# Up-projection weight sums made in earlier stages, a fixed engine order in the up stage, and a down stage laid into the slots that the up stage frees

## The chip, the cores and the metric

One core of one Trainium2 chip runs the whole kernel. The metric is the device time of one execution in microseconds (us). A profiled execution also has a span, from its first to its last instruction, and times inside the trace are counted from the start of that span. The engines are named as in the profile: PE is TensorE's matrix multiply and PEld its weight load, DVE is VectorE, ACT is ScalarE, POOL is GpSimd, and SP is the queue that only issues transfers.

## What is computed

One layer of a streaming encoder for 1024 prompt tokens and 8 x 16 sample tokens, together T = 1152 columns. Up to the feed-forward part:

```python
h = rms_norm(x, g_norm_mix);  z = h @ w_in              # latents, retention q k v, gates ga and gb
attn = latent_attention(...);  ret = retention(...)
merged = sigmoid(ga) * (attn @ w_oA) + sigmoid(gb) * (ret @ w_oR)
x = x + merged @ w_out
```

and the part that the change is mostly about, the convolutional feed-forward with D = 1024 and D_FF = 2816:

```python
u  = rms_norm(x, g_norm_ffn) @ w_ffn_up                 # 1024 -> 2 * 2816, gate and value halves
up = concatenate([prev, u], axis=1)                     # two earlier tokens of each sequence
c  = up[:, 0:T] * cw[0] + up[:, 1:T+1] * cw[1] + up[:, 2:T+2] * cw[2] + w['ffn_conv_b']
gate, val = c[..., :D_FF], c[..., D_FF:]
x  = x + (jax.nn.silu(gate) * val) @ w_ffn_down
```

All of it is float32. The kernel writes each operand as a rounded part `hi` and a rest `lo`, and makes a product from three matrix multiplies (hi hi, hi lo, lo hi).

## The kernel before

Features stand on the 128 partitions and tokens along the free dimension. The stages follow one another: the gates ga and gb with the first norm (lines 356 to 412), latent keys and values, retention, queries, keys and the sample tokens, prompt attention (lines 1048 to 1131, eight heads), the merge (lines 1183 to 1272: three layers `w_or`, `w_oa`, `w_out` of eight output tiles each), the up stage (lines 1278 to 1406) and the down stage (lines 1411 to 1454). Tile's scheduler puts the instructions of each engine into one fixed list before the launch: it may move an instruction ahead of others on its engine, by its own estimate of when operands and buffers are there. On the chip each list then runs in order, so an instruction that waits holds up all behind it on that engine. `tc.issue_after(i)` and `tc.add_manual_dep` bind the scheduler to an order on one engine.

`split` (line 203) makes the two parts of a tile: ACT copies `hi`, DVE subtracts `lo`.

**Attention.** For each head, POOL issues the loads of `aq`, `ak` and `av` (lines 1107 to 1110, two buffers each). PE makes scores `sc` in four banks, DVE takes maxima, ACT exponentials `ap`, DVE scales them (`L1073`), PE transposes and multiplies with the values. SP has hardly anything to issue.

**Merge.** `bslot` (line 1156) loads a weight tile into one of two raw buffers `wr` and splits it. The first weights of `w_or` depend on nothing of attention; their buffers lie where the weight pool of the stages before was.

**Up stage.** Gate tile j and value tile j form a pair, 22 pairs in all. A pair is a 2 x 2 block product done with seven block products instead of eight; `products` (line 1296) runs them in the order `p q p q r q r` over three pairs of accumulation banks, 24 matrix multiplies of 288 columns each. The seven left operands need sums of four half weights, s1 to s4. `up_w` (line 1278) loads both raw weight tiles of the next pair, has POOL make the four sums (lines 1283 to 1286), and splits seven half tiles. `read` (line 1345) takes the banks out: r1 and c11 by ACT, the others by DVE with a subtraction or an addition. After the pair `scaled` (line 1366) has POOL put the earlier tokens in, multiply by the norm's factor `ivx` and keep the last tokens; `conv` (line 1374) makes the three taps (one on ACT, two on DVE, for gate and for value), then ACT's Silu, DVE's product, and two stores of `s_act` from ACT's queue. The scheduler mixes this with the next pair's work. The second norm (line 1319) begins one step into pair 0.

**Down stage.** It has pools of its own. For each of three column groups of 384 tokens and eight output tiles, 22 k-steps of three matrix multiplies run into one bank. `down_w` loads and splits a weight tile in three pieces (two sets), `down_a` loads and splits 22 activation tiles one by one through ACT's queue.

## Time and profile before

| what | us |
|---|---|
| median of 3 runs | 2501.18 |
| fastest, slowest run | 2500.33, 2502.37 |
| the profiled execution's own time | 2497.31 |
| its span | 2495.5 |
| PE busy | 2398.6 (96%) |
| PEld busy | 2278.9 (91%) |
| DVE busy | 1488.1 (60%) |
| ACT busy | 961.9 (39%) |
| POOL busy | 605.0 (24%) |

The mean granted clock of TensorE is 0.983 of full speed. An engine's busy share here is a mean over stages with quite different limits, so the reading goes by stage: a table of stretches of the span, then the list of what PE waited for, then single instructions with their start and length. A time behind "idle before" or in square brackets is how long the engine stood idle, with the instruction that released it.

### The profile page before, as it was taken

How to read it: one execution, taken by the hardware profiler on the slowest of the kernel's cores; microseconds unless marked ns; L12 is line 12 of the kernel's file. 1: busy time of each engine (PE TensorE's matmuls, PEld its weight loads, DVE VectorE, ACT ScalarE, POOL GpSimd, SP SyncE). 2: the span in 40 equal slices, each digit the busy share in tenths (PEclk: the TensorE clock that was granted, in tenths of full speed). 3: DMA queues.
4: the chain of work that ended last, by engine and by line, in shares of the span. 5: the costliest groups of instructions: out<-in, count | busy, mean ns of one | idle time of the engine just before them, and what ended most of it. 6: DMA issues, size and time to landing. Idle time of an engine off the chain costs nothing.

```text
span 2495.5 us, 38305 instructions
## 1 busy us (share of the span) xinstructions
PE 2398.6 (96%) x14888; PEld 2278.9 (91%) x14888; DVE 1488.1 (60%) x2792; ACT 961.9 (39%) x2294; POOL 605.0 (24%) x678
## 2 busy tenths in 40 slices
PE   9999999999999999996999999999999999959999
PEld 8999998898999978885999999989999999959999
DVE  6223456546259766444886244579999998855432
ACT  5121332333246555663665022443333333344321
POOL 0001001001013212331110000237677676510000
PEclk9999999999999999998999999999999999979999
DMA  5333220111125666327674342532212222158653
GB/s 198 102 109 116 79 72 20 62 64 41 65 89 177 207 236 204 113 81 192 184 198 134 107 147 90 170 125 75 74 63 71 71 72 70 63 187 264 217 160 90
DMA packets 153893, 303.02 MB, mean 121 GB/s; under 512 B 13392, under 2 KB 88528, under 8 KB 153456
## 3 DMA queue, kind: packets, MB, share of 16 engines
q1 hardware_dynamic: 51552, 159.64, 19.7%
q10 hardware_dynamic: 74096, 88.26, 10.3%
q0 software_dynamic: 28064, 52.67, 7.5%
q8 instruction: 117, 1.92, 0.3%
q14 instruction: 64, 0.52, 0.1%
HBM read 212.47 MB, written 88.06 MB: 120 GB/s over the span
## 4 chain that ended last, share of the span: by engine, by line
PE 76%; DVE 10%; ACT 4%; DMA 4%; issue 4%; POOL 3%; ACTq 0%; SPq 0%; POOLq 0%; DVEq 0%
PE mm L188 56%; PE mm L1308 7%; PE sm L188 4%; PE sc L188 3%; POOL ug L1370 3%; PE apo L188 2%; DVE cg L1377 2%; DVE wlo L206 1%; DVE cv L1376 1%; PE apt L1085 1%; ACT whi L205 1%; DVE cg L1376 1%; ACT cg L1375 1%; DMA ar<-s_act 1%; DMA s<-s_ret 1%
## 5 line engine op out<-in xcount | busy, mean ns | idle before, releaser
L206 DVE TENSOR_TENSOR wlo<-wraw,whi 128x1024 fp32r<-128x1024 f32 (+2 forms) x165 | 232.2, 1415 | 149.9 <-ACT whi L205 149.8
L205 ACT CAST whi<-wraw 128x1024 fp32r<-128x1024 f32 (+2 forms) x165 | 162.6, 993 | 388.0 <-PE mm L188 286.1
L1308 PE MATMUL mm<-xt,whi 128*128 128x288 f32 x1408 | 287.5, 298 | 11.9 <-DVE u L1351 10.8
L188 PE MATMUL mm<-act,dh 128*128 128x384 f32 x1056 | 272.2, 338 | 26.9 <-ACT act L205 26.9
L1308 PEld LDWEIGHTS mm<-xt,whi 128*128 128x128 f32 x1408 | 224.6, 188 | 20.0 <-DVE u L1351 15.4
L188 PE MATMUL mm<-whi,xh 128*128 128x256 f32 (+2 forms) x720 | 228.4, 334 | 0.7 <-DVE gsig L365 0.7
L188 PE MATMUL mm<-whi,xl 128*128 128x256 f32 (+2 forms) x720 | 225.5, 330 | 0.0
L188 PE MATMUL mm<-wlo,xh 128*128 128x256 f32 (+2 forms) x720 | 225.0, 329 | 0.3 <-DVE wlo L206 0.3
L1308 PE MATMUL mm<-xb,whi 128*128 128x288 f32 x1056 | 215.6, 298 | 9.6 <-ACT r L1349 9.6
L188 PEld LDWEIGHTS mm<-act,dh 128*128 128x128 f32 x1056 | 192.3, 189 | 30.9 <-ACT act L205 29.2
L1308 PE MATMUL mm<-xt,wlo 128*128 128x288 f32 x704 | 207.8, 295 | 0.0
L1308 PEld LDWEIGHTS mm<-xb,whi 128*128 128x128 f32 x1056 | 170.2, 189 | 14.7 <-ACT r L1349 14.4
L188 PE MATMUL mm<-act,dl 128*128 128x384 f32 x528 | 177.2, 337 | 0.0
L1308 PE MATMUL mm<-xb,wlo 128*128 128x288 f32 x528 | 156.4, 296 | 0.0
L188 PEld LDWEIGHTS mm<-whi,xl 128*128 128x128 f32 x720 | 132.7, 190 | 12.1
L188 PEld LDWEIGHTS mm<-whi,xh 128*128 128x128 f32 x720 | 132.8, 190 | 10.5 <-issue 0.7
L188 PEld LDWEIGHTS mm<-wlo,xh 128*128 128x128 f32 x720 | 132.8, 190 | 9.8 <-DVE wlo L206 0.5
L206 DVE TENSOR_TENSOR dl<-dr,dh 128x1024 fp32r<-128x1024 f32 (+1 forms) x72 | 81.5, 1136 | 94.1 <-ACT dh L205 90.0
L188 PE MATMUL mm<-rh,whi 128*128 128x384 f32 x576 | 131.9, 336 | 2.0 <-ACT rh L205 2.0
L188 PE MATMUL mm<-rl,whi 128*128 128x384 f32 x576 | 132.1, 336 | 0.4 <-DVE rl L206 0.4
L1308 PEld LDWEIGHTS mm<-xt,wlo 128*128 128x128 f32 x704 | 132.3, 188 | 0.1
L188 PE MATMUL mm<-rh,wlo 128*128 128x384 f32 x576 | 131.5, 335 | 0.0
(481 smaller groups left out, 5787.7 us busy)
## 6 DMA issues: line engine op xcount, KB each, us to landing
dr<-w_dn SPq DMA_DIRECT2D x48, 512.0 KB, 3.6
wraw<-w_up SPq DMA_DIRECT2D x44, 512.0 KB, 3.4
s_q<-uqT ACTq DMA_DIRECT2D x36, 384.0 KB, 3.1
ar<-s_act ACTq DMA_DIRECT2D x66, 192.0 KB, 3.6
aq<-s_q POOLq DMA_DIRECT2D x8, 1536.0 KB, 8.7
s_act<-cv ACTq DMA_DIRECT2D x22, 512.0 KB, 2.6
s_gate<-gsig ACTq DMA_DIRECT2D x16, 576.0 KB, 4.8
mg<-s_gate POOLq DMA_DIRECT2D x16, 576.0 KB, 4.7
```

Of the source, the lines that this page charges most:

```text
L188: E.matmul(out, l, r, start=start, stop=stop)
L205: A.copy(hi, src)
L206: return V.tensor_tensor(out=lo, in0=src, in1=hi.bitcast(F32), op=ALU.subtract)
L1085: E.transpose(pt[:, j * 256 + e * P:j * 256 + (e + 1) * P], pm[e][:, jj * P:(jj + 1) * P], ident)
L1308: E.matmul(banks[bank][c], l[:, ks], x, start=bool(first) and k + e == 0, stop=k + e == 5, skip_group_check=not first)
L1370: G.tensor_tensor(out=u[:, 2:], in0=u[:, 2:], in1=ivx[:, 2:], op=ALU.mult)
L1375: A.activation(c, u[:, 2:], AF.Identity, scale=gc(C_CW, 2 * NF + f), bias=gc(C_CB, f))
L1376: V.scalar_tensor_tensor(out=c, in0=u[:, 1:NU - 1], scalar=gc(C_CW, NF + f), in1=c, op0=ALU.mult, op1=ALU.add)
L1377: V.scalar_tensor_tensor(out=c, in0=u[:, 0:NU - 2], scalar=gc(C_CW, f), in1=c, op0=ALU.mult, op1=ALU.add)
```

## The change

- `presum(j, pool, bufs)` loads the two raw up weights of pair j from SP's queue, makes the four sums on POOL, and stores them to a new scratch tensor `s_w[j]` (1 MB each) from POOL's queue. Pairs 0 to 10 are made in the gate stage, one per gate tile 2 to 12 with two buffers; pairs 11 to 21 in attention, one or two per head, with one buffer for each raw tile.
- `up_raw` loads the finished sums beside the raw weights into four raw buffers of their own; the up stage makes no sums.
- The second norm starts after product 4 of pair 0 instead of near its beginning.
- From pair 1 on, `in_order` chains ACT's, DVE's and POOL's instructions in the order in which they are written. The convolution of pair j-1 is written into the products of pair j. Multiplying by `ivx` moves from POOL to DVE, in three pieces, and into the reading of c11, which moves from ACT to DVE.
- `s_act` holds three pairs in a tile and is stored from SP's queue.
- The splits of the first two `w_or` weights are bound behind the last ACT and DVE instructions of head 5.
- The down stage takes slots of the up stage. In the last pair it loads and splits its first weights and activations; the first two output tiles run side by side, k-step by k-step; the rest of the last pair's convolution is written between their splits, in a fixed order. Activations are loaded three at a time from POOL's queue.

```diff
+        def presum(j, p, bufs):
+            rg, rv = (p.tile([P, D], F32, name=n, bufs=bufs) for n in ("prg", "prv"))
+            S.dma_start(rg, d["w_up"][j])
+            S.dma_start(rv, d["w_up"][NJ + j])
+            s = p.tile([P, 4, 512], F32, name="psum", bufs=2)
+            u, v = slice(0, 512), slice(512, D)
+            G.tensor_tensor(out=s[:, 1], in0=rg[:, u], in1=rv[:, u], op=ALU.add)
...
+            G.dma_start(s_w[j], s)
...
                     gate_out(f, fm_tile(mm, wslot(d["w_gate"][f], D), xr))
+                    presum(f - 2, wk, 2)
...
+                for j in range(11 + 11 * h // H, 11 + 11 * (h + 1) // H):
+                    presum(j, wk, 1)
...
+                if h == H - 3:
+                    anchors = [next(i for i in reversed(nc.cur_bb.bb.instructions) if i.engine == e) for e in (mybir.EngineType.Activation, mybir.EngineType.DVE)]
...
-            wts = [bslot(d[w][f]) for f in (f0, f1)]
+            with ExitStack() as block:
+                if not turn[0]:
+                    for i in anchors:
+                        block.enter_context(tc.issue_after(i))
+                wts = [bslot(d[w][f]) for f in (f0, f1)]
...
+        def up_raw(j):
+            return [wraw(0, d["w_up"][j]), wraw(1, s_w[j][:, 0:2]), wraw(2, s_w[j][:, 2], d["w_up"][NJ + j][:, 512:]), wraw(3, s_w[j][:, 3])]
...
+            def then(n, ps):
+                g, v = j - 1, NJ + j - 1
+                if n == 0:
+                    me.read_p(ps)
+                    if prev:
+                        prev.keep(g, prev.ug)
+                        prev.tap(v, prev.uv, prev.cv, 1)
+                elif n == 1:
+                    me.read_u2(ps)
+                    if prev:
+                        prev.tap(v, prev.uv, prev.cv, 0)
+                        prev.tap(g, prev.ug, prev.cg, 1)
+                        prev.tap(g, prev.ug, prev.cg, 0)
+                        A.activation(prev.cg, prev.cg, AF.Silu)
+                    if last:
+                        me.ra = [act_raw(0, i) for i in range(3)]
+                elif n == 2:
+                    me.read_c11(ps)
+                    if last:
+                        wa.extend(down_w(0, 0, set_a))
+                    else:
+                        prep(0)
+                    if prev:
+                        prev.product()
+                elif n == 3:
+                    me.read_u3(ps)
...
+                        prep(1)
+                elif n == 4:
+                    me.read_c22(ps)
+                    me.past(NJ + j, me.uv)
+                    if j:
+                        me.scale(me.uv, A2)
...
+                elif n == 5:
+                    me.read_c21(ps)
+                    if j:
+                        me.scale(me.uv, A1)
+                        me.keep(NJ + j, me.uv)
+                        me.cv = me.tap2(NJ + j, me.uv, "cv")
...
+                        prep(2)
                 else:
+                    me.read_c12(ps)
+                    me.past(j, me.ug)
+                    if j:
+                        me.scale(me.ug, A2)
+                        me.cg = me.tap2(j, me.ug, "cg")
+                    if not last:
+                        prep(3)
...
+            with in_order():
+                prev.keep(j, prev.ug)
+                acts += act_split(prev.ra[2], act_tiles(AT[2]))
+                ra = [act_raw(0, i) for i in (3, 4)]
+                prev.tap(v, prev.uv, prev.cv, 1)
+                prev.tap(v, prev.uv, prev.cv, 0)
+                wa += down_w(0, 1, set_a)
+                prev.tap(j, prev.ug, prev.cg, 1)
+                prev.tap(j, prev.ug, prev.cg, 0)
+                A.activation(prev.cg, prev.cg, AF.Silu)
+                wb += down_w(1, 1, set_b)
+                acts += act_split(ra[0], act_tiles(AT[3]))
+                ra += [act_raw(0, i) for i in (5, 6)]
+                prev.product()
...
+            for k in range(NJ):
+                for q, ww in zip(ps, (wa, wb)):
+                    mm3(q, ww[k], acts[k], k == 0, k == NJ - 1)
```

`tap` is one DVE tap of 1168 columns, `tap2` ACT's tap with the bias, `prep(i)` the split of the next pair's raw tile i (1024, 1024, 1024 and 512 columns), `scale` the multiplication by `ivx`, `past` and `keep` small POOL copies of the earlier and the last tokens.

## Rows read from the trace of the kernel before

**Rows 1.** What PE waited for, whole span: total us, times, longest.

```profile
PE mm L188 <- ACT act L205: 26.9, 5, 24.9
PE sc L188 <- ACT ap L1069: 14.8, 2, 14.2
PE mm L1308 <- DVE u L1351: 10.8, 20, 0.6
PE mm L1308 <- ACT r L1349: 9.6, 21, 1.7
PE sm L315 <- DVE acc L1234: 5.0, 1, 5.0
```

**Rows 2.** Stretches: A:B, length, PE, PEld, DVE, ACT, POOL busy, PEclk, DMA share, GB/s.

```profile
0.00:40.00 40.00, 37.00 (x200) 35.35 (x201) 26.80 (x28) 28.17 (x30) 1.13 (x6) 1.00 0.64 214
914.50:917.90 3.40, 3.40 (x15) 3.30 (x16) 1.66 (x4) 1.50 (x6) 0.98 (x1) 0.50 0.62 196
1190.00:1337.00 147.00, 147.00 (x1060) 139.43 (x1058) 122.79 (x395) 94.17 (x286) 19.48 (x24) 1.00 0.63 169
1640.00:1684.00 44.00, 37.97 (x242) 36.53 (x241) 34.10 (x48) 20.02 (x31) 16.95 (x14) 0.88 0.25 80
1700.00:2160.00 460.00, 440.96 (x3229) 429.53 (x3228) 416.98 (x425) 164.89 (x210) 327.56 (x268) 1.00 0.20 69
2072.00:2076.00 4.00, 2.35 (x18) 2.12 (x18) 3.80 (x4) 1.64 (x2) 3.94 (x6) 1.00 0.08 31
2184.00:2240.00 56.00, 29.13 (x136) 25.36 (x136) 27.98 (x37) 22.23 (x32) 6.46 (x9) 0.73 0.57 180
2240.00:2490.00 250.00, 250.00 (x1442) 249.54 (x1441) 106.24 (x133) 82.11 (x109) 11.27 (x21) 1.00 0.61 188
```

**Rows 3.** By line, shapes apart: least/median/longest ns, or busy us and mean ns.

```profile
L1377 DVE SCALAR_TENSOR_TENSOR cv<-uv,c_gcol,cv x22: 1430/3901/3908, 1686.0 to 2187.6; 128x1168 f32<-128x1168 f32 x22
L1375 ACT ACTIVATE cv<-uv,c_gcol x22: 1360/1366/1369, 1682.2 to 2184.5; 128x1168 f32<-128x1168 f32 x22
L1283 POOL TENSOR_TENSOR wsum<-wraw x22: 1287/2421/2431, 1614.7 to 2145.6; 128x512 f32<-128x512 f32 x22
L206 DVE TENSOR_TENSOR wlo<-wraw,whi 128x1024 fp32r<-128x1024 f32 x8 | 9.7, 1218 | 6.0 <-ACT whi L205 6.0
L205 ACT CAST whi<-wraw 128x1024 fp32r<-128x1024 f32 x40 | 42.0, 1051 | 56.2 <-PE mm L1308 56.2
```

**Rows 4.** In order of time, the start of attention: start, length, instruction.

```profile
1159.00 1.04 ACT L205 CAST whi<-wraw 128x1024 fp32r<-128x1024 f32 x1 [10.28 <-DMA s_att<-wraw]
1163.52 1.23 DVE L206 TENSOR_TENSOR wlo<-wraw,whi 128x1024 fp32r<-128x1024 f32 x1 [2.22 <-ACT whi L205]
```

**Rows 5.** In order of time, ACT's Silu in pairs 1 and 21.

```profile
1694.00 1.18 ACT L1399 ACTIVATE cg<-cg 128x1168 f32<-128x1168 f32 x1 [2.34 <-DVE cg L1377]
2172.46 1.18 ACT L1399 ACTIVATE cg<-cg 128x1168 f32<-128x1168 f32 x1 [2.97 <-DVE cg L1377]
```

**Rows 6.** In order of time, PE within a pair of the up stage.

```profile
1812.41 0.29 PE L1308 MATMUL mm<-xt,wlo 128*128 128x288 f32 x1
1812.81 0.29 PE L1308 MATMUL mm<-xt,wlo 128*128 128x288 f32 x1
1813.63 0.53 PE L1308 MATMUL mm<-xt,whi 128*128 128x288 f32 x2 [0.53 <-DVE u L1351]
```

**Rows 7.** In order of time, DVE reading banks one behind the other.

```profile
1796.70 0.44 DVE L1338 TENSOR_TENSOR uv<-u,mm 128x288 f32<-128x288 f32 x1
1797.07 0.31 DVE L1341 TENSOR_TENSOR uv<-u,mm 128x160 f32<-128x160 f32 x1
1797.30 0.28 DVE L1343 TENSOR_TENSOR uv<-u,mm 128x128 f32<-128x128 f32 x1
```

**Rows 8.** By line, attention 1190 to 1337: one shape of the scaling.

```profile
L1073 DVE TENSOR_SCALAR ap<-ap,ast 128x1024 f32<-128x1024 f32 x7 | 5.5, 780 | 0.0
```

**Rows 9.** In order of time, PE ahead of the second stretch of rows 2.

```profile
914.34 0.44 PE L188 MATMUL sm<-vh,sl 128*128 128x256 f32 x1 [1.51 <-DVE sl L206]
```

More of the change, by code (lines that the diff above doesn't have):

```diff
@@ L201, in behind, with __enter__, __exit__ @@
         return block
+    class in_order:
+        def __enter__(self):
+            self.at = len(nc.cur_bb.bb.instructions)
+        def __exit__(self, *_):
+            traced = nc.cur_bb.bb.instructions
+            for e in (mybir.EngineType.Activation, mybir.EngineType.DVE, mybir.EngineType.Pool):
+                last = None
+                for n, i in enumerate(traced):
+                    if i.engine != e:
+                        continue
+                    if n >= self.at and last is not None:
+                        tc.add_manual_dep(i, last.name, mybir.DependencyInfo(mybir.DependencyClass.NoSync, mybir.DependencyReason.DATA), reason="in_order")
+                    last = i
     def split(hi, lo, src, scale=None):
@@ L316, in col_sums @@
             return ps[:, :NT]
+        def presum(j, p, bufs):
[5 more added lines that the diff above has]
+            G.tensor_tensor(out=s[:, 1], in0=rg[:, u], in1=rv[:, u], op=ALU.add)
+            G.tensor_tensor(out=s[:, 2], in0=rv[:, u], in1=rv[:, v], op=ALU.add)
+            G.tensor_tensor(out=s[:, 0], in0=s[:, 2], in1=rg[:, u], op=ALU.add)
+            G.tensor_tensor(out=s[:, 3], in0=s[:, 0], in1=rg[:, v], op=ALU.add)
+            G.dma_start(s_w[j], s)
         warm = ExitStack()
@@ L1308, in products @@
                             E.matmul(banks[bank][c], l[:, ks], x, start=bool(first) and k + e == 0, stop=k + e == 5, skip_group_check=not first)
-                    read(n, c, banks[bank][c])
-                stream.tick()
+                then(n, banks[bank])
         us = ExitStack()
@@ L1379, in _body @@
-        w = up_w(0)
-        stream.now = 0
-        nrm = norm()
-        def later():
-            yield 1
-            yield from nrm
-        stream.start(later())
-        for j in range(NJ):
-            ug, uv = up(j, w)
-            stream.drain()
-            if j < NJ - 1:
-                w = up_w(j + 1)
-            scaled(NJ + j, uv)
-            cv = wk.tile([P, NU - 2], F32, name="cv")
-            conv(NJ + j, uv, cv)
-            scaled(j, ug)
-            cg = wk.tile([P, NU - 2], F32, name="cg")
-            conv(j, ug, cg)
-            A.activation(cg, cg, AF.Silu)
-            V.tensor_tensor(out=cv[:, :SEQ], in0=cg[:, :SEQ], in1=cv[:, :SEQ], op=ALU.mult)
-            sa = wk.tile([P, NB * NS], F32, name="sa")
-            sv = lambda a: a[:, SEQ:].rearrange("p (b c) -> p b c", c=NS + 2)[:, :, 2:]
-            V.tensor_tensor(out=sa.rearrange("p (b i) -> p b i", b=NB), in0=sv(cg), in1=sv(cv), op=ALU.mult)
-            A.dma_start(s_act[j][:, :SEQ], cv[:, :SEQ])
-            A.dma_start(s_act[j][:, SEQ:], sa)
@@ new lines, in act_split, with act_tiles @@
+        def act_split(r, two):
+            n = r.shape[1]
+            hi, lo = (t.rearrange("p (a c) -> p a c", a=3)[:, :n] for t in two)
+            split(hi, lo, r)
+            return [(hi[:, i], lo[:, i]) for i in range(n)]
+        def act_tiles(tags):
+            return [slots.tile([P, T], F32R, name="act", tag=t) for t in tags]
+        AT = [(5, 6), (7, 8), (9, 10), (13, 14), (15, 16), (19, 20), (21, 22), (23, 24)]
+        AT = [tuple(DS[i] for i in t) for t in AT]
+        raw_w = up_raw(0)
```

305 lines of the change are left out of this document (193 added, 112 removed).

## The prediction

> **What bounds the kernel now.** I read the table of stretches first, then the list of what PE waited for, then single instructions. PE is busy in 96% of the span, so a change can win only where PE stands still or runs at its lower clock. The list of waits puts most of that into two places: 26.9 us for the down stage's first activations and 14.8 us for attention's exponentials [rows 1]. The up stage adds 20.4 us in small waits, one for r1 and one for u2 in each pair, and the second norm 5.0 us [rows 1]. In the table attention and the down stage hold PE busy throughout at full clock, while 2184 to 2240 has 136 matrix multiplies and a clock of 0.73, and 1640 to 1684 a clock of 0.88 [rows 2]. In the up stage DVE is as full as PE, 417 of 460 us, because POOL is busy 328 us beside it [rows 2]: the same DVE tap takes 1.43 us at least and 3.90 us in the median, POOL's addition 1.29 and 2.42 [rows 3]. The longer ones are those that meet the other engine.
>
> **Start of attention.** ACT's copy of a `w_or` weight waited 10.3 us for a transfer that waited for the store of `s_att` [rows 4]. Its partner on DVE ended at 1164.75, and attention's first maxima and exponentials stand behind both; hence PE's 14.2 us. Binding these splits behind head 5 removes that, and their cover there is two heads of full PE work. The third weight of `w_or` is not bound and could still stand in front, for one load and one split (about 4 us, estimated from the 1.05 and 1.22 of its parts and a load). I take 12 us won, between 8 and 17 (the whole wait, and some 2 us of lower clock behind it).
>
> **Up to down.** In 2184 to 2240, 136 multiplies at 250/1442 = 0.173 us are worth 23.6 us; 32 us are lost [rows 2]. Afterwards PE can start at once: the first weights and six activations are split within the last pair. The two outputs side by side use a k-step in 6 x 0.173 = 1.04 us, so k = 8 is wanted 8.3 us after the last up product. What is needed then stands in a fixed order on DVE and ACT: reading c12 and scaling (1.8), ACT's tap (1.37), activation group 2 (1.16 and 1.36, by columns from 1.05 and 1.22), two taps, a weight piece, two taps (2.8, 1.15, 2.8), Silu (1.18), the other piece (1.05 and 1.22): 15.9 us, with some 2 us that DVE is behind, and then activations 9 to 11 (1.4). That is 19 us against the 9.4 at which k = 9 is wanted. So about 11 us are lost in waits, and 2.7 more at the lower clock. Won: 32 - 13.5 = 18.5 us, between 12 and 27. The conv_new store, the POOL-issued activation loads and the y stores ride beside 12 us of multiplies per output, as now.
>
> **Merge to up.** `col_sums` no longer stands in front of PE at 5.0 us [rows 1]; the norm's work itself stays and goes between products 4 to 6 and pair 1, where scaling and ACT's taps of pair 0 hold r1 of pair 1 for 1 to 2 us. I take 4 won, 1 to 7.
>
> **Up stage.** A pair takes (2172.46 - 1694.00)/20 = 23.92 us [rows 5]. PE's own pace is three multiplies in 0.40 us, 56 x 0.398 = 22.3 [rows 6]. Without POOL's sums and scalings DVE's operations fall to their least times, but they stand in a fixed order now. Per pair: four taps 5.72 [rows 3]; eight bank reads of 0.44 and two sets of 0.44 + 0.31 + 0.28 [rows 7], 5.58, c11 among them; three scalings of 576 to 592 columns, about 0.76 each between 128 and 1024 columns, 2.28; four rests 3 x 1.22 + 0.68, 4.34 [rows 3]; the product 1.5. Together 19.4, less 0.07 where an operation starts before the one ahead has ended [rows 7], about 1.4: 18.0 us. In that order DVE waits three times for ACT. Behind the last tap: Silu 1.18 and a copy 1.05, less the reading of c11, 1.5. Behind the second scaling: ACT's tap 1.37 and a copy 1.05, 2.4. Behind the third: 1.37 and 0.6, 2.0 [rows 3, 5]. That is 5.9 and 0.2 for the steps between engines: 24.1 us a pair. So the stage goes from DVE with POOL to a loop through DVE and ACT, and PE waits once a pair, about 1.8 us, at product 5 for u3, instead of twice. Behind DVE's waiting subtraction stand the reads of c12 and u3, and PE for their banks. 21 pairs at +0.15: 3 us lost, between 28 won (PE's pace) and 10 lost (the loop 0.5 us longer). POOL's copies fit in DVE's waits; s_act on SP's queue and four loads a pair meet a DMA share of 0.20 [rows 2].
>
> **Sums in the gate stage.** 44 POOL additions and 22 MB of transfers move here. SP waits for raw buffers after the first x rows, so I expect the first four loads (2.1 MB, buffers are free from the start) ahead of the later x rows in SP's queue. The stretch 0 to 40 moves 214 GB/s at a share of 0.64 [rows 2], so 2.1 MB are some 6 us of the full rate, and the additions (1.29 each) meet DVE, which splits x for PE. Bounds: nothing, if PE's rows come in time; 14 for both. I take 6, nearer to the transfers. The stage behind it has DVE mostly free, and a gate tile of 72 multiplies lasts 12.5 us.
>
> **Sums in attention.** PE is full there and DVE busy 122.8 of 147 us [rows 2]. 44 additions of 1.29 us are on POOL 57 of 190 us. The 64 scalings (1024 columns in 0.78 us [rows 8]) and as many tiny two-input operations of the softmax may each meet one with a chance of 0.3 and wait half of it: 25 us of DVE at most, which would fill it to 97%. The transfers add 23 MB in 190 us, 121 GB/s; at the down stage's 0.61 for 188 GB/s [rows 2] that is 0.39 beside 0.63: the queues would be full, and POOL's loads of the next heads share them. They have a whole head, 22 us, to come. Bounds 0 and 25; I take 7, nearer to PE's full rows.
>
> The Trainium skill says on this (SBUF — State Buffer, section "SBUF: two separate sides") that DVE, with two SBUF inputs or in a two-port mode, and GpSimd hold a shared port pair as "an exclusive lock, not a bandwidth split", for a whole instruction. The trace agrees: 3.90 against 1.43 us. By that rule alone the up stage would fall to PE's pace and attention would pay the full 25 us; the sum would be 2466 for the execution.
>
> **Sum.** 2497.3 - 12 - 18.5 - 4 + 3 + 6 + 7 = 2478.8 for an execution like the profiled one; the median of the runs is 3.9 above that execution, so 2482.7; I give 2482.
>
> **Rivals.**
> - *The up stage reaches PE's pace.* For it: DVE's 18.0 us of work fit in 22.3, and the scheduler may still move PE and SP. Against it: ACT's and DVE's orders are fixed, and the three waits stand in the text. 22.3 to 22.6 a pair: 31 us less than the forecast, 2452.
> - *Slower: PE's one wait drops the clock.* A wait of 1.5 us was followed by 3.4 us at 0.50, the 1.2 GHz level [rows 2, 9]; one of 1.7 us in the up stage was not, the clock stayed at 1.00, 2.4 GHz [rows 1, 2]. With 1.8 us in every pair it could go either way. 3.4 us at half clock cost 1.7 us a pair, 36 in all: 2519. It decides from about 15 pairs of 21.
> - *The sums cost what they save.* Gate and attention at their upper ends, 39 us instead of 13: 2509. For it: a full DMA share and a full DVE. Against it: none of this is needed before the up stage.
> - *The bound splits don't free attention*, since other work is put in front of it: 12 us back, 2495.
>
> **How the numbers follow.** The forecast has 0.55, PE's pace 0.13, the clock 0.11, the costly sums 0.16, the missing anchor 0.05. The forecast's own range is 2466 to 2497. To leave out no more than 0.2 the range goes down to PE's pace, 2451, and up to the costly sums, 2508. About 0.2%, 5 us, is what a measurement can tell from no change. Faster: nearly all of the forecast, PE's pace, and half of the missing anchor, 0.70. Same, 2496 to 2506: half of the costly sums, half of the missing anchor and the forecast's upper end, 0.13. Slower: the clock and the rest of the sums, 0.17.
>
> **What would show it.** Right: no wait of PE near 1150 us; a wait of 5 to 8 us some 9 us into the down stage and full rows after; Silu every 24 us; DVE's taps at 1.43; one PE wait for u3 per pair. Wrong: a period of 22.5 (DVE not the loop), a PEclk under 1.00 between 1700 and 2160, waits for x rows in the first 30 us above 14, or scores waiting for `ak` and `aq` in attention.

## The result and the profile after

The changed kernel takes 2513.0 us (median of 4 runs, 2511.9 to 2515.4) against 2500.8 us before: a ratio of 1.005, interval 1.0032 to 1.0067. It is slower by 0.5%, where 2482 us were forecast. Its profiled execution took 2511.9 us, 14.6 more than the one of before.

Where that came from is seen first in the positions of a few TensorE instructions, in us from the start of the span. (The last column is the start of the last multiply of the down stage. The lower rows belong to experiments below.)

| kernel | end of the kv stage | first score | end of attention | first up product | last down product |
|---|---|---|---|---|---|
| before | 241.8 | 1148.1 | 1341.1 | 1645.5 | 2491.6 |
| after | 259.0 | 1166.1 | 1367.8 | 1671.6 | 2506.0 |
| no sums in the gate stage | 244.2 | 1153.8 | 1355.0 | 1660.7 | 2492.9 |
| no sums in attention | 258.6 | 1166.0 | 1351.6 | 1657.0 | 2489.7 |
| gate sums, transfers alone | 256.1 | 1163.2 | 1365.1 | 1669.9 | 2500.9 |
| gate sums held back | 249.0 | 1159.0 | 1361.4 | 1665.7 | 2500.4 |
| taps moved | 260.5 | 1168.8 | 1367.6 | 1672.4 | 2457.8 |
| no order, sums late | 246.7 | 1164.6 | 1342.1 | 1647.3 | 2424.3 |

So the changed kernel is 17.2 us behind when the kv stage ends, and between there and the first score it loses only 0.8 more. Attention takes 201.6 us instead of 192.9. From the end of attention on it is faster by 12.3.

From the list of what PE waited for, whole span, columns as in [rows 1]:

```profile
PE mm L1342 <- ACT whi L222: 18.8, 19, 1.0
PE mm L1342 <- DVE wlo L223: 8.8, 19, 0.5
PE sc L188 <- ACT ap L1101: 7.4, 2, 5.2
PE mm L188 <- DVE gsig L396: 6.4, 4, 5.0
PE sm L327 <- DVE diag L324: 6.0, 1, 6.0
PE apo L188 <- DVE apT L223: 5.4, 11, 0.6
PE mm L188 <- ACT dwhi L222: 4.5, 1, 4.5
PE mm L188 <- ACT act L222: 3.6, 2, 3.0
PE apo L188 <- DMA av<-s_v: 3.6, 2, 2.4
```

The two large lines of [rows 1] have shrunk: the down stage's activations from 26.9 to 3.6 and 4.5 (weights), attention's exponentials from 14.8 to 7.4. New are the two single waits of the gate stage, of 5.0 and 6.0 us, the small ones in attention, and one line that was not in the forecast: 19 waits of 1.0 us for the copy of the next pair's weights in the up stage.

Four stretches that answer to [rows 2], by stage and moved with the work, and the stretch 40 to 90 beside them:

```profile
0.00:40.00 40.00, 34.78 (x177) 32.59 (x178) 31.75 (x23) 25.07 (x27) 19.40 (x15) 0.96 0.76 267
40.00:90.00 50.00, 39.03 (x204) 36.55 (x203) 24.08 (x31) 12.41 (x13) 35.05 (x30) 0.90 0.93 355
1215.00:1362.00 147.00, 140.01 (x971) 131.09 (x971) 126.95 (x367) 88.10 (x267) 60.90 (x59) 0.98 0.91 277
1725.00:2185.00 460.00, 432.63 (x3180) 422.88 (x3179) 341.13 (x510) 148.36 (x171) 43.16 (x152) 1.00 0.31 101
2205.00:2261.00 56.00, 44.98 (x240) 42.20 (x239) 40.71 (x47) 25.88 (x26) 11.53 (x21) 0.88 0.61 208
```

In the up stage POOL fell from 328 to 43 busy us in 460, DVE from 417 to 341, and yet PE starts 3180 multiplies where it started 3229. In the seam to the down stage PE has 240 multiplies in 56 us instead of 136. The first two lines show the price of the gate's sums. The fullest transfers of that stage are not in its first 40 us but behind them, 355 GB/s at a share of 0.93, and there PE is busy 39 of 50 us, at a clock of 0.90.

Two single waits of PE, of 6.0 and 5.0 us, are all that is missing there. In order of time on SP, ACT, DVE, POOL and PE (start, length, instruction, in brackets the idle time ahead of it and what ended it):

```profile
11.54 0.75 SPq L339 DMA_DIRECT2D prg<-w_up  x1
13.67 0.65 SPq L340 DMA_DIRECT2D prv<-w_up  x1
39.55 1.51 SPq L282 DMA_DIRECT2D wraw<-w_gate  x3
46.66 1.04 ACT L222 CAST whi<-wraw 128x1024 fp32r<-128x1024 f32 x1 [9.37 <-DMA wraw<-w_gate]
47.73 1.22 DVE L223 TENSOR_TENSOR wlo<-wraw,whi 128x1024 fp32r<-128x1024 f32 x1 [6.44 <-ACT whi L222]
49.13 1.83 POOL L278 TENSOR_TENSOR inv<-ss,negh 128x9 f32<-128x9 f32 x1 [2.82 <-DVE ss L434]
51.81 1.65 PE L327 MATMUL sm<-diag,ones 128*128 128x384 f32 x2 [5.98 <-DVE diag L324]
54.45 2.75 DVE L324 TENSOR_SCALAR diag<-ident,inv 128x128 f32<-128x128 f32 x3
64.19 2.31 DVE L223 TENSOR_TENSOR wlo<-wraw,whi 128x1024 fp32r<-128x1024 f32 x1
78.89 1.49 DVE L396 TENSOR_TENSOR gsig<-mm,ivb 128x384 f32<-128x384 f32 x3 [10.36 <-DMA s_gate<-gsig]
79.50 1.61 PE L188 MATMUL mm<-xh,whi 128*128 128x384 f32 x3 [4.99 <-DVE gsig L396]
```

The first four loads of the sums were issued at 11.5 to 13.7 us, ahead of later x rows, as forecast; that cost some 3 us (the norm's first column sum starts at 40.4 instead of 37.4). The wait of 6.0 us came from SP's queue. After 30.7 SP waited 8.4 us to issue a load of the sums, because its tile was still read by POOL's additions, which took 2.1 to 2.4 us each beside DVE's work instead of 1.29 [rows 3]; the loads of the next gate weights stood behind it and went out from 39.55 on. ACT's copy of such a weight waited for its load until 46.66, DVE's rest for that copy, and DVE's reading of the norm's column sums, ready since 42.6, stood behind that rest until 48.88. POOL itself was idle then, and its `inv` took 1.83 us. Behind it DVE's diagonals and rests take two to four times their length beside the next additions (2.31 instead of 1.22 [rows 3]), and DVE waits 10.4 us until a store of `s_gate` gives its tile back, with PE behind it.

### The profile page after: what moved, and what is told of

Its sections match the earlier page's. It is cut to its first block, busy times and chain, and to the rows that moved or that the text cites. A ratio compares the mean times of both kernels' runs of the same rounds, so it can differ in the third digit from the quotient of the medians.

```text
span 2510.1 us, 38500 instructions
## 1 busy us (share of the span) xinstructions
PE 2406.2 (96%) x14888; PEld 2284.6 (91%) x14888; DVE 1441.6 (57%) x2857; ACT 938.8 (37%) x2210; POOL 436.1 (17%) x679
## 4 chain that ended last, share of the span: by engine, by line
PE 68%; DVE 15%; DMA 6%; issue 5%; ACT 4%; POOL 2%; ACTq 0%; SPq 0%; DVEq 0%; POOLq 0%
PE mm L188 54%; PE mm L1342 5%; PE sm L188 4%; DVE wlo L223 3%; ACT whi L222 2%; DVE cg L1432 2%; DVE cv L1432 2%; DMA prg<-w_up 2%; PE sc L188 1%; PE apo L188 1%; DVE ug L1420 1%; DMA prv<-w_up 1%; DVE uv L1420 1%; DVE u L1381 1%; DMA ak<-s_k 0%
## 5 line engine op out<-in xcount | busy, mean ns | idle before, releaser
L223 DVE TENSOR_TENSOR wlo<-wraw,whi 128x1024 fp32r<-128x1024 f32 (+4 forms) x223 | 261.3, 1178 | 312.0 <-ACT whi L222 310.9
L222 ACT CAST whi<-wraw 128x1024 fp32r<-128x1024 f32 (+4 forms) x223 | 217.9, 993 | 416.9 <-PE mm L188 349.8
L188 PE MATMUL mm<-act,whi 128*128 128x384 f32 x528 | 136.2, 337 | 4.6 <-ACT act L222 3.6
L188 PE MATMUL mm<-act,dwhi 128*128 128x384 f32 x528 | 135.7, 336 | 4.5 <-ACT dwhi L222 4.5
L188 PE MATMUL mm<-xh,whi 128*128 128x384 f32 x528 | 125.1, 343 | 8.7 <-DVE gsig L396 5.7
L188 PE MATMUL mm<-xl,whi 128*128 128x384 f32 x528 | 122.3, 337 | 1.1 <-DVE xl L226 1.1
```

The source lines that it names most:

```text
L188: E.matmul(out, l, r, start=start, stop=stop)
L222: A.copy(hi, src)
L223: return V.tensor_tensor(out=lo, in0=src, in1=hi.bitcast(F32), op=ALU.subtract)
```

## The experiments

Each was made from the changed kernel unless it says otherwise, and its ratio is to the kernel before, run beside it on the same chip.

### Without the gate's sums, without attention's

```diff
-                    presum(f - 2, wk, 2)
...
+            q = j % 11 + 11
-            return [wraw(0, d["w_up"][j]), wraw(1, s_w[j][:, 0:2]), wraw(2, s_w[j][:, 2], d["w_up"][NJ + j][:, 512:]), wraw(3, s_w[j][:, 3])]
+            return [wraw(0, d["w_up"][j]), wraw(1, s_w[q][:, 0:2]), wraw(2, s_w[q][:, 2], d["w_up"][NJ + j][:, 512:]), wraw(3, s_w[q][:, 3])]
```

> The changed kernel without the eleven sets of sums of the gate stage; pairs 0 to 10 of the up stage read the sums of pairs 11 to 21 instead, so the up stage has the same loads and the same work but other numbers. Theory 'the sums cost what they save' (stage boundaries after the gate stage stand 17 us later in the changed kernel than before): the kernel gets 14 to 19 us faster, 2494 to 2499 us, and the boundary at the end of the kv stage falls back to that of the kernel before within 2 us. Rival 'the shift comes from the order in which the scheduler put the gate stage's own work, not from the sums': under 5 us, 2508 to 2513.

Measured: 2494.6 us, ratio 0.9977 (0.9968 to 0.9986). The kv stage ends at 244.2, 2.5 us from before (2 were forecast).

```diff
-                for j in range(11 + 11 * h // H, 11 + 11 * (h + 1) // H):
-                    presum(j, wk, 1)
...
+            q = j % 11
```

> The changed kernel without the eleven sets of sums of the attention stage; pairs 11 to 21 read the sums of pairs 0 to 10. Theory 'the sums stand in the way of attention' (its body lost some 15 us, its start won 6): 10 to 20 us faster, 2493 to 2503 us, and the start of attention wins the 12 us that the forecast gave it, because the head transfers of the sums no longer stand beside it. Rival 'attention lost to the anchored weight loads and the third split that is bound to nothing': within 3 us, 2510 to 2516.

Measured: 2495.9 us, 0.9985 (0.9975 to 0.9995). Attention takes 185.6 us: 16.0 less than with the sums, but only 7.3 less than before. So the sums cost 18 and 17 us of the whole time, 35 if the two add up, and the first theory held in both; that the start of attention would get back its 12 us did not come true. Something else stands there.

### What of the sums it is, in the gate stage

```diff
+            if j < 11:
+                G.dma_start(s_w[j][:, 0:2], rg)
+                G.dma_start(s_w[j][:, 2:4], rv)
+                return
             s = p.tile([P, 4, 512], F32, name="psum", bufs=2)
```

> The changed kernel with the gate stage's sums reduced to their transfers: the same two loads, and stores of the same 8 KB per partition taken straight from the loaded tiles, with no addition on POOL (so pairs 0 to 10 multiply other numbers). Theory 'transfers': the loads at 11 to 14 us push the x rows back and fill the queue, and the 17 us stay within 4 us, 2509 to 2513 us. Rival 'the shared port of DVE and POOL': the additions alternate with DVE's row splits and evacuations, and most of it goes, 10 to 16 us, 2497 to 2503.

Measured: 2506.6 us, 1.0023 (1.0013 to 1.0034): 6 us won, between the two forecasts, 2.9 of them up to the end of the kv stage. Transfers alone keep 14.3 of the 17.2 us there, but not at the same places. The stretch 40 to 90, and DVE behind it in order of time:

```profile
40.00:90.00 50.00, 49.21 (x282) 47.32 (x281) 16.55 (x32) 14.77 (x15) 7.75 (x12) 1.00 0.96 361
111.34 0.76 DVE L462 TENSOR_TENSOR c_cos<-c_cos,c_grow 128x576 f32<-128x576 f32 x1 [27.40 <-DMA c_grow<-grow]
112.69 1.48 DVE L400 TENSOR_TENSOR gsig<-mm,ivb 128x384 f32<-128x384 f32 x3
```

In 40 to 90 PE now loses almost nothing, with as many bytes as in the changed kernel (361 and 355 GB/s): the two waits there need the additions as well. The constants that the kv stage multiplies are loaded from SP's queue too. DVE came to them early in its own order, waited 27.4 us for their transfer, and the gate's evacuation stood behind it; PE waited 6.8 us. That the loss is one of waiting in order was not what I had expected. How much of the 17 us belongs to the bytes and how much to the additions this run does not tell, since the waits moved; and the edit does one thing more: a tile that is stored as it was loaded is free only when its store has landed.

```diff
-                    presum(f - 2, wk, 2)
+                    with behind():
+                        presum(f - 2, wk, 2, A)     # loads from ACT's queue
```

> The changed kernel with each set of the gate stage's sums loaded from ACT's queue behind that gate tile's sigmoid, so that the first loads start after the norm instead of at 11 us; the same sums, the same number of bytes. Theory 'it is where they start': the 17 us shrink to 0 to 5, 2496 to 2501 us, with no gap of PE above 2 us between 50 and 90 us. Rival 'the sums cost this wherever they lie in this stage': over 10 of the 17 us stay, 2506 to 2513.

Measured: 2499.8 us, 1.0007 (0.9995 to 1.0019), 13 us won with the same bytes and the same additions. The stretch 40 to 90 is whole again, and a new wait stands at 201.6, of DVE and PE in order of time:

```profile
40.00:90.00 50.00, 49.35 (x284) 48.23 (x284) 16.70 (x31) 12.53 (x13) 16.03 (x11) 1.00 0.62 214
199.70 0.76 DVE L459 TENSOR_TENSOR c_cos<-c_cos,c_grow 128x576 f32<-128x576 f32 x1 [3.29 <-DMA c_grow<-grow]
201.61 0.40 PE L188 MATMUL mm<-whi,xh 128*128 128x288 f32 x1 [3.27 <-DVE ckv L475]
```

So most of the cost was in where the loads stand, as the theory had it. The edit changes two things at once, when the loads start and whose queue they are in: SP's queue no longer waits for POOL ahead of a gate weight. Which of the two did it is not separated. What remains lies at the end of the gate stage, where SP waits 7.3 us for the last additions ahead of a load of the kv stage's constants, and DVE for such a transfer.

### What of the sums it is, in attention

```diff
+            if j >= 11:
+                G.dma_start(s_w[j][:, 0:2], rg)
+                G.dma_start(s_w[j][:, 2:4], rv)
+                return
```

> The changed kernel with the attention stage's sums reduced to their transfers: the same two loads, and stores of the same bytes straight from the loaded tiles, no addition on POOL (so pairs 11 to 21 multiply other numbers). Without any of it the stage won 17 us. Theory 'the transfers fill the queues' (the heads' own loads and the first weights come late, as in the gate stage, where the transfers alone kept 14 of 17 us): under 5 us are won, 2508 to 2513 us. Rival 'the shared port': DVE is busy for 88 % of this stage and each addition shuts it out, so 10 to 16 us are won, 2497 to 2503 us.

Measured: 2520.4 us, 1.008 (1.006 to 1.010): without the additions it is 7 us slower than with them, which neither forecast had. What PE waited for between 1185 and 1375:

```profile
PE sc L188 <- DMA aq<-s_q: 8.2, 1, 8.2
PE sc L188 <- DMA ak<-s_k: 3.4, 1, 3.4
PE apo L188 <- DMA av<-s_v: 2.4, 1, 2.4
```

In the changed kernel the same list has 5.0 us for `apT`, in ten waits, and 4.0 for `av` and `ak`. The additions therefore cost PE some 5 us through DVE (0.3 us are left here); but without them 14 us are waited for the heads' own loads. These are issued from POOL's queue, behind whatever waits there for a load of the sums: an addition in the changed kernel (first fence), a store in this one (second).

```profile
1290.89 1.28 POOL L343 TENSOR_TENSOR psum<-prg,prv 128x512 f32<-128x512 f32 x1 [6.16 <-DMA prg<-w_up]
1295.67 1.81 POOL L1142 DMA_DIRECT2D av<-s_v  x2
```

```profile
1288.34 0.56 POOL L342 DMA_DIRECT2D s_w<-prg  x1 [8.43 <-DMA prg<-w_up]
1289.59 0.77 POOL L1143 DMA_DIRECT2D aq<-s_q  x1
```

Between 1185 and 1310 POOL waited 111 us for loads of the sums in this run and 48 in the changed kernel. As in the gate stage, a tile is held here until its store has landed, so the loads themselves are not the same in time, and why the run is slower than with the additions is not settled.

To tell the queue from the bandwidth, the same bytes with the stores from SP:

```diff
-                G.dma_start(s_w[j][:, 0:2], rg)
-                G.dma_start(s_w[j][:, 2:4], rv)
+                S.dma_start(s_w[j][:, 0:2], rg)
+                S.dma_start(s_w[j][:, 2:4], rv)
```

> As the run with attention's sums reduced to their transfers, with the stores issued from SP's queue instead of POOL's: the same bytes, but POOL's queue, from which the heads' own loads are issued, never waits for a load of the sums. (Pairs 11 to 21 multiply other numbers.) Against that run's 2520 us. Theory 'queue order': the waits for aq, ak and av (14 us in that run) go, and the time falls by 10 to 18 us, 2502 to 2510 us. Rival 'bandwidth': the queues of the transfer engines are full in this stage, and the heads' loads stay late, 2516 to 2523 us.

Measured: 2522.4 us, 1.0088 (1.0071 to 1.0105). By the time the rival holds, by the trace neither. No wait for `aq`, `ak` or `av` is left. In their place PE waits 16.7 us for ACT's `apT` and 11.9 for ACT's `aat`, and ACT waits, between 1160 and 1260:

```profile
ACT whi L222 <- DMA wraw<-w_or: 17.0, 1, 17.0
ACT ap L1105 <- DMA prv<-w_up: 15.2, 1, 15.2
```

The first is the third weight of the merge, whose load is now queued on SP behind the stores that wait. The second names a load of the sums; ahead of it ACT issued a store of `s_att` (at 1249.28, after 14.9 us without an instruction), and what held that is not settled. So moving the 11.5 MB of stores to another queue moved the wait to whoever shares that queue. How much of attention's 16 us would stay if nothing stood behind the sums in any queue, these runs do not say.

### The start of attention

```diff
-                ps = fm_tile(mm, bslot(d[w][f]), rows) if i > 1 else first[i]
+                if i > 1:
+                    with bound():          # behind the anchors while turn[0] < 3
+                        wt = bslot(d[w][f])
+                ps = fm_tile(mm, wt, rows) if i > 1 else first[i]
...
+        with bound(99):
             w = [wtile(r, r.shape[1], i) for i, r in enumerate(raw_w)]
```

> The changed kernel with the third weight split of the merge and the first pair's four splits bound to the same two instructions of head 5 as the first two. In the changed kernel the third split stands on ACT ahead of attention's first exponential and waits 6.0 us for its weights. Theory 'that one split is what is left of the wait at the start of attention': TensorE's 5.6 us gap there shrinks to at most 1.5, and with the half clock behind it 6 to 9 us are won, 2504 to 2507 us. Rival 'the transfers of attention's sums are late anyway': under 2 us, 2511 to 2514 us.

Measured: 2506.7 us, 1.0030 (1.0018 to 1.0041), 6 us won. On ACT in order of time, first the changed kernel (its two splits are the third weight of `w_or` and the last of the first pair), then this one:

```profile
1172.67 1.71 ACT L222 CAST whi<-wraw 128x1024 fp32r<-128x1024 f32 x2 [5.96 <-DMA wraw<-w_or]
1174.28 0.36 ACT L1101 ACTIVATE ap<-sc,ast 128x128 f32<-128x128 f32 x1
```

```profile
1169.28 0.37 ACT L1101 ACTIVATE ap<-sc,ast 128x128 f32<-128x128 f32 x1 [0.93 <-DVE ast L1094]
```

PE's gap in the scores goes from 5.2 to 1.1 us, and the time is in the range of the theory. Attention as a whole gets 2.9 us shorter in the two profiles (198.7 us): a wait of 3.6 us for `ak`, and two stretches of 6.8 us at the 1.2 GHz level (a granted clock of 0.50), took part of it back. The other side of the test, the kernel before with nothing but the three splits bound:

```diff
-            wts = [bslot(d[w][f]) for f in (f0, f1)]
+            with bound():
+                wts = [bslot(d[w][f]) for f in (f0, f1)]
```

> The kernel before with only one part of the change, extended by its missing third: the first three weight splits of the merge bound behind head 5. The forecast gave 12 us, between 8 and 17. Theory 'the wait at the start of attention is those splits and nothing else': 12 to 15 us won against the kernel before, 2485 to 2489 us. Rival 'the first scores wait for something else next' (as with the changed kernel's sums left out, where 7 us came of it): 5 to 9 us, 2491 to 2496 us.

Measured: 2487.7 us, 0.9947 (0.9932 to 0.9962), 13.5 us won; attention falls from 192.9 to 178.2 us, and no wait of PE above 1 us is left between the first score and 1190. The theory holds: the splits were the whole wait, and all three must be bound.

### The up stage

The period from Silu to Silu, over 20 pairs, is (2206.7 - 1719.7)/20 = 24.35 us in the changed kernel (23.92 before [rows 5]). By line, shortest/median/longest ns and first and last start:

```profile
L1515 ACT ACTIVATE cg<-cg x21: 1179/1180/1182, 1719.7 to 2206.7; 128x1168 f32<-128x1168 f32 x21
```

One pair, in order of time, on PE, ACT and DVE:

```profile
1794.82 0.80 PE L1342 MATMUL mm<-xb,whi 128*128 128x288 f32 x4 [0.99 <-ACT whi L222]
1796.08 0.40 PE L1342 MATMUL mm<-xb,wlo 128*128 128x288 f32 x1 [0.47 <-DVE wlo L223]
1792.65 1.18 ACT L1515 ACTIVATE cg<-cg 128x1168 f32<-128x1168 f32 x1 [6.40 <-DVE cg L1432]
1793.74 1.98 ACT L222 CAST whi<-wraw 128x1024 fp32r<-128x1024 f32 x2
1805.09 1.23 DVE L223 TENSOR_TENSOR wlo<-wraw,whi 128x1024 fp32r<-128x1024 f32 x1 [2.41 <-ACT whi L222]
1809.99 0.69 DVE L223 TENSOR_TENSOR wlo<-wraw,whi 128x512 fp32r<-128x512 f32 x1 [2.00 <-ACT whi L222]
1810.60 1.43 DVE L1432 SCALAR_TENSOR_TENSOR cv<-uv,c_gcol,cv 128x1168 f32<-128x1168 f32 x1
```

The taps have their 1.43 us, and DVE waits for ACT where it was forecast, 2.4 and 2.0 us. PE however waits for the next pair's weights: the written order binds ACT, DVE and POOL, and the scheduler placed 18 of the next pair's 24 first multiplies ahead of this pair's last two products.

```diff
-                for e in (mybir.EngineType.Activation, mybir.EngineType.DVE, mybir.EngineType.Pool):
+                for e in (mybir.EngineType.Activation, mybir.EngineType.DVE, mybir.EngineType.Pool, mybir.EngineType.PE):
```

> The changed kernel with the written order of the up stage fixed for TensorE too, and nothing else. In the changed kernel the scheduler put 18 of the next pair's first 24 matmuls ahead of this pair's last two products, and TensorE waits there 1.0 us for the copy of the next weights. Theory 'the loop of DVE and ACT sets the period': the wait of 1.3 us moves to the reads of the next pair, the period stays between 24.0 and 24.4 us and the time within 6 us, 2507 to 2515. Rival 'TensorE's order sets the period': it falls to 22.5 to 23.0 us, and the time by 27 to 38, 2475 to 2486 us.

Measured: 2512.7 us, 1.0050 (1.0033 to 1.0066), the same as the changed kernel. PE between 1740 and 2140:

```profile
PE mm L1342 <- DVE u L1381: 26.9, 16, 1.9
```

Now PE waits once a pair for u3, 1.7 us, just as the forecast said, and the period is 24.27. PE's order decides where it waits, not how long the pair is. The loop itself:

```diff
 # product 0 of the next pair
-                        prev.tap(v, prev.uv, prev.cv, 1)
 # product 1
-                        prev.tap(v, prev.uv, prev.cv, 0)
...
-                        A.activation(prev.cg, prev.cg, AF.Silu)
 # product 2, behind prep(0)
+                        A.activation(prev.cg, prev.cg, AF.Silu)
 # product 6 of the own pair, behind the tap on ACT
+                        me.tap(NJ + j, me.uv, me.cv, 1)
+                        me.tap(NJ + j, me.uv, me.cv, 0)
```

> The changed kernel with DVE's two taps of the value half moved from the head of the next pair to the end of its own pair, where DVE waits 2.0 us for ACT, and the copy of the next weights put ahead of Silu on ACT. Same work. Theory 'the period is the loop from the last read of a pair over the scaling, ACT's tap, DVE's four taps and Silu to the next weights': the loop loses 2.7 us and the period falls to TensorE's own, 22.3 to 22.7 us, 2472 to 2482 us. Rival 'something else sets it' (the exclusive port, or the weights' transfers): above 23.9 us a pair, 2503 to 2513 us.

Measured: 2464.7 us, 0.9860 (0.9846 to 0.9875), 48 us won, more than the theory's range; it beats both kernels. And the order taken away altogether:

```diff
-                    if n >= self.at and last is not None:
+                    if n < 0:
```

> The changed kernel with the written engine order of the up stage and of its tail taken away: the scheduler places the same work. The forecast's term for the up stage was 24.1 us a pair with the order written out; measured 24.30. Theory 'the written order is what lengthens the pair': the scheduler moves the value half's taps into DVE's idle time by itself, as the moved taps did by hand, and the period falls to 22.4 to 23.2 us, 2470 to 2490 us. Rival 'the order costs nothing, the sums' removal had already made the loop': 23.9 to 24.5 us, 2506 to 2518 us.

Measured: 2459.5 us, 0.9837 (0.9813 to 0.9861), again more than forecast. The stretch 1725 to 2150 of the changed kernel, of the taps moved, and of no order, each in its own fence:

```profile
1725.00:2150.00 425.00, 400.17 (x2944) 391.36 (x2943) 314.84 (x473) 136.23 (x156) 39.48 (x142) 1.00 0.32 102
```

```profile
1725.00:2150.00 425.00, 425.00 (x3210) 425.00 (x3209) 345.98 (x520) 152.06 (x171) 51.31 (x156) 1.00 0.34 111
```

```profile
1725.00:2150.00 425.00, 425.00 (x3210) 425.00 (x3209) 352.33 (x520) 159.69 (x172) 68.09 (x152) 1.00 0.34 111
```

In both PE has no gap left: 425 us hold 3210 multiplies, and 425/3210 x 168 = 22.2 us for a pair. The written order, not the work, was the limit of the changed up stage. With DVE's taps at the head of the next pair, each pair runs through the last read, the scaling, ACT's tap, four taps and Silu before the next weights are copied, 24.3 us in all; two taps moved into DVE's wait of 2.0 us, and Silu put behind the copy, take the loop under PE's own pace. (The run makes both moves, so their shares are not known.)

The order cost something behind the pairs too. From the same multiply of the last pair to the last one of the down stage, the kernel with the taps moved takes 298.0 us and the one without the order 289.7. There PE has no wait above 0.4 us, at a clock of 1.00; with the order it waited 3.6 us for a piece of a down weight, and the clock stood at 0.50 for 6.8 us behind it.

### The sums somewhere else

```diff
-                    presum(f - 2, wk, 2)
+                    if f < 12:
+                        with behind():
+                            presum(f - 2, wk, 2, A)
...
+                    for hf in range(2):                      # query latents
+                        with behind():
+                            presum_half(10 + f, hf, wk, A)
...
+                    for hf in range(2):                      # first layer of the merge
+                        with behind():
+                            presum_half(todo[0], hf, wk, A)
```

> The changed kernel with the same 22 sets of sums made elsewhere: ten in the gate stage, loaded from ACT's queue behind each gate tile's sigmoid from the third tile on; six in halves in the stage of the query latents; six in halves under the first layer of the merge; none in the attention stage. Theory 'the cost of the sums is that of the place': gate 0 to 5 us instead of 17, attention the 16 back, 2480 to 2490 us. Rival 'their 63 MB and 88 additions cost the same wherever they lie': above 2505 us.

Measured: 2580.9 us, 1.0320 (1.0303 to 1.0337), the worst of all, though attention took 184.3 us. PE waited for these, among others:

```profile
PE mm L188 <- ACT rh L222: 25.0, 3, 16.8
PE mm L188 <- DVE upn L736: 23.8, 1, 23.8
776.50 0.28 ACT L725 ACTIVATE usq<-mm 128x128 f32<-128x128 f32 x1 [32.88 <-DMA s_w<-prg]
```

With single buffers an addition on POOL waits for each load, and a load on ACT's queue until the store of the half before has landed. The 23.8 us for `upn`, from 762 on, show both: ACT's squares for that tile stood behind such loads until 776.5 (the last line, a row of ACT in time), and then POOL's powers until 783.8, behind a half whose first addition had waited 5.2 us for `prg`. The time lies in the rival's open range, but 68 us above the changed kernel is not "the same", and neither theory had this: here the cost hung less on the bytes, or on a stage being idle, than on what is queued behind each wait.

```diff
+            V.tensor_tensor(out=s[:, v], in0=rg[:, u], in1=rv[:, u], op=ALU.add)   # additions on DVE
...
+                    with behind():
+                        nxt = presum(f - 2, wk, A)         # loads behind this gate tile
+                        next(nxt)
+                    if f > 2:
+                        next(held_sum)                      # additions one tile later
...
+                        if t in (0, 3) and todo:            # retention stage, raw weight buffers
+                            mine = presum_in(todo.pop(0))
```

and, with it, the moved taps and the bound splits of above.

> Everything that the earlier runs point to, in one kernel: the taps moved and the weights' copy ahead of Silu in the up stage, the third split and the first pair's splits bound, the sums of pairs 0 to 10 in the gate stage with loads from ACT's queue behind each gate tile and additions on DVE one tile later, those of pairs 11 to 21 in the retention stage, through the weights' own raw buffers, additions on DVE. Theory 'three separate causes that add up': the taps' 48 us, the split's 6, 14 to 17 of the gate's and 16 to 17 of attention's: 2424 to 2436 us. Rival 'the sums cost in the retention stage too', because its weight loads share the three buffers and the queue: 10 to 25 us more, 2436 to 2455 us.

Measured: 2450.6 us, 0.9803 (0.9783 to 0.9823): the rival's range, some 20 us short of the sum. One wait of 14.5 us is in the gate stage, on DVE and PE:

```profile
189.62 0.69 DVE L338 TENSOR_TENSOR psum<-prg,prv 128x512 f32<-128x512 f32 x1 [7.99 <-DMA prv<-w_up]
192.98 0.82 PE L188 MATMUL mm<-whi,xh 128*128 128x288 f32 x2 [14.50 <-DVE gsig L413]
```

The scheduler had put each addition ahead of the evacuation; the addition waits for its load, the evacuation for the addition, the next load for that tile's sigmoid. It is the same fault again. The retention stage was not free either: from the end of the kv stage to the first score this kernel takes 921.0 us, where the kernel before takes 906.3 and the changed one 907.1.

```diff
-                    if f > 2:
-                        next(held_sum)
+                    if f > 2:
+                        with behind():                      # behind this tile's evacuation
+                            next(held_sum)
...
-                    if n >= self.at and last is not None:
+                    if n < 0:                               # no written order
```

> The changed kernel without the written engine order, with the third split and the first pair's splits bound, ten sets of sums in the gate stage (loads from ACT's queue behind each gate tile, additions on DVE behind the next tile's evacuation, so that an addition that waits for its load holds no evacuation up) and twelve in the retention stage as in the combined kernel. Theory 'the combined kernel lost its 15 us gap at 178 us to the place of the additions on DVE, and 9 us behind the up stage to the written order of its tail': 2418 to 2432 us. Rival 'the gate stage has no room for the sums': 2436 to 2452 us.

Measured: 2428.5 us, 0.9718 (0.9702 to 0.9734): 2.8% faster than before and in the range of the theory, with the same sums made outside the up stage. Attention takes 177.5 us, and the kv stage ends at 246.7. From there to the first score it is 917.9 us: the twelve sets in the retention stage still cost some 11 us, and the ten in the gate stage 5.

## Why the prediction was wrong

**The two terms for the sums failed, and with them the sign.** Gate +6 and attention +7 were forecast; the positions give +17.2, and the runs without them 18 and 17 us of the whole time. That is the rival "the sums cost what they save", 2509, which had 0.16.

- *In the gate stage* the mechanism of the step was right as far as it went: four loads ahead of the later x rows, some 3 us. It stopped at 40 us. "The stage behind it has DVE mostly free" looked at an engine's share and left out the queues: the gate weights' loads share SP's queue with loads that wait for POOL's additions, and the norm on DVE stands behind those weights (a wait of 6.0); and a gate tile's buffer comes free by a store which rides in the same full transfers (5.0). I took the stretch 0 to 40 as the place of collision, though the loads run on as fast as buffers allow; the upper bound of 14 was too low as well. Loading later and from ACT's queue, with the same bytes and additions, won 13 us.
- *In attention* +7 stood between 0 and 25, reasoned over DVE's share. Without the sums attention is 16.0 us shorter. The additions cost PE some 5 us by that way, near the step's 7. The step put nothing beside it for what shares a queue with the sums: "they have a whole head, 22 us, to come" priced the heads' loads by their bandwidth, and not by where they are issued, behind an addition that waits for a load. PE waited 4.0 us for them, and behind the wait for `av` the granted clock stood at 0.50, the 1.2 GHz level, for 6.8 us, some 3 us more. The last 3 of the 16 us are in no single wait, and their cause stays open.

**Start of attention, -12: mechanism right, and undone at the point named.** The third weight, put at "about 4 us", stood in front as feared, for 6.0 us and two splits; without the sums 7.3 us were won. With all three bound the kernel before won 13.5. The step should have asked what the scheduler does with a split that nothing binds; here it stood ahead of attention's first exponential. So the rival that other work is put in front, which had 0.05, came in good part.

**Up stage, +3.** Forecast 24.1 us a pair, measured 24.35: 21 x 0.43 = 9 us lost instead of 3. (By the step's own numbers it is 0.18 a pair, 3.8 us, not 0.15.) The loop through DVE and ACT was the right one, and the wait for u3 appears as soon as PE keeps its order. The place of PE's wait was wrong, since PE was free to be scheduled. The rival "PE's pace" failed as the changed kernel stands; but it was worth more than I gave it, as two taps moved gave 48 us. The clock rival did not come: waits of 1.0 and 0.5 us in every pair left the granted clock at 1.00, the 2.4 GHz level.

**Merge, up to down, -22.5: right in the main.** From the end of attention on 12.3 us are won; with the 9 lost in the pairs that leaves 21.3. Taken at the same multiplies in both kernels, some 4 of it are won up to pair 2, as forecast, and 16 from the last pair on, instead of 18.5. (The sum of that step slipped: 19 less 9.4 is 9.6 and not 11, and 11 with 2.7 is 13.7 and not 13.5; put right, it gives 19.7 won.) The wait that it left in was the price of the fixed order, as the run without it shows. The wait in the down stage came as two, of 4.5 us for a weight piece and 3.0 for an activation, with a mean clock of 0.88 over the 56 us of the seam instead of 0.73 [rows 2].

Put together: 11 us missed in the gate stage, 14 in attention with its start, 6 in the pairs and 1 in the seam make 32, and 2479 + 32 = 2511 against the 2512 of the execution.

The Trainium skill (SBUF — State Buffer, section "SBUF: two separate sides") has the shared port of DVE and GpSimd as an exclusive lock. The trace agrees where it can be seen: 2.31 us for a rest of 1.22 beside an addition. The sum that went by that rule alone, 2466, was further off than mine, as it takes the up stage to PE's pace and knows no order.

The Trainium skill also says (DMA: Bandwidth & Descriptors, section "Issuing engines are not separate DMA queues") that transfers issued by different engines run on the same 16 DMA engines, and that using several only saves the time to initiate them. For the bytes this case agrees: with stores from SP instead of POOL the stretch 1215 to 1362 moved 257 GB/s instead of 268, and the time stayed within 2 us (2520.4 and 2522.4). But the choice of queue decided which instruction waited: 14 us for the heads' loads in one run, 28.6 us behind ACT in the other.

## What to carry to other kernels

Work that is moved to a stage "where there is room" is priced by what stands behind it in each in-order queue it passes, its loads, its additions and its stores each for itself, and less by its bytes or its share of an engine; hold its loads back until the stage's own start is over and out of the queue of the stage's own weights, and put what consumes them behind the stage's own urgent instructions. An order written out by hand is a loop: add up the steps from the last read of one round to the first need of the next before trusting it, and try the kernel without it. Binding TensorE as well changed where it waited and not the round (24.27 us); dropping the order won 53 us. When part of a group of instructions is bound behind an anchor, look for the next of the group that is not.

## What the hardware showed that was not expected

Fewer instructions beside the same bytes did not make attention faster: with POOL's 44 additions taken out, the time rose by 7 us, and the heads' own loads came later (PE waited 8.2 us for `aq`), behind stores that waited for the loads of the sums. And in a burst single transfers took longer: in the stretch 40 to 90 the changed kernel moved 355 GB/s, and the gate's stores of 576 KB issued there took 9.9 us in the median from issue to landing. It was 4.6 us at 133 GB/s before, and 3.4 at 214 GB/s with the sums held back.
